# Hybrid encoder layer: head outputs kept in SBUF, scan operands laid out by step, local attention by bias class, stabilisers and norms moved into the first stage

## The chip, the cores and the metric

The kernel runs on one core of a Trainium2 chip. The metric is the device time of one execution in microseconds (us). A profile shows one execution: its span runs from the first to the last instruction.

## The reference

One layer of a bidirectional encoder over 2048 tokens of width 1024. All three head groups read one normalised input through one projection; then follow the output projection, cross attention to 256 memory tokens and a squared-ReLU MLP.

```python
h = rmsnorm(x, norm_mix_w[l])
(na_q, na_k, na_v, ml_q, ..., gd_b, gd_a) = jnp.split(h @ w_in[l], IN_OFFSETS, axis=-1)
y_na = neighbourhood_attention(na_q, na_k, na_v, na_rel_bias[l])    # 6 heads, window 8 x 16 on a 32 x 64 grid
y_ml = mlstm_mixer(...)                    # 4 heads; out = head_rms(h_fwd + h_bwd) * norm_w * sigmoid(o_pre)
y_gd = gated_deltanet_mixer(...)           # 6 heads; o = head_rms(o_fwd + o_bwd) * norm_w * silu(z)
x = x + jnp.concatenate([y_na, y_ml, y_gd], axis=-1) @ w_out[l]
x = x + memory_cross_attention(rmsnorm(x, ...), rmsnorm(mem, ...), w_xq[l], w_xkv[l], w_xo[l])
h = rmsnorm(x, norm_ffn_w[l])
x = x + jnp.square(jax.nn.relu(h @ w_ff1[l])) @ w_ff2[l]
# gdn_direction, one chunk of 64 tokens:
v_new = u_c - jnp.einsum('bhld,bhde->bhle', w_c, state)
o = jnp.einsum('bhld,bhde->bhle', qd_c, state) + jnp.einsum('bhls,bhse->bhle', a_c, v_new)
state = state * jnp.exp(gl_c)[..., None, None] + jnp.einsum('bhld,bhle->bhde', ks_c, v_new)
```

The mLSTM has the same form with a matrix memory and a running maximum (its stabiliser). Both scans run once forwards and once backwards, and the two outputs are added before the head norm.

## The kernel before

The kernel has three stages. `pass_a` normalises the input in four blocks of 512 tokens (`norm_in`), runs the projections as three-pass split GEMMs (the helper at L95: weights and activations are split into a high and a low part, `whi` and `wlo`), the convolution and gates of the gated DeltaNet (GDN), and its Gram matrices and inverses. GEMM work of the other groups is a generator, `fill`, advanced between steps of that chain. `norm_in(2)` and `norm_in(3)` were called between pieces of `fill`. What `pass_b` needs is written to DRAM: `sc_d`, `g_row`, `v_d`, `w_d` and `gd_c` for the GDN, `mlc_d`, `mlv_d` for the mLSTM, `nac_d`, `nav_d` for local attention, `gate_d` for the output gates.

`pass_b` interleaves four generators: 16 steps of the GDN scan (`gdn_scan`), 16 steps of the mLSTM scan one step later (`ml_scan`), local attention over 16 blocks of 128 tokens (`na`), and the head outputs (`heads_out`). A step handles 128 tokens of each direction: the forward scan takes tile m, the backward scan tile 15 - m. `load(m + 1)` is issued ahead of step m. Its DMAs all go through the SyncE queue, which runs in order. The scheduler moves instructions between generators, so the order on each engine is not that of the code. `ml_prep` computes the running-max stabilisers ahead of the mLSTM scan and writes rows `mx_row` and `ai_row`.

The two directions sit in the two halves of the 128 partitions (`CH[d]`). A row that all 64 partitions need, as `ge` or `me`, is read from DRAM once for each partition:

```python
nc.sync.dma_start(out=kb[CH[d]], in_=self.sc_d[d, t, :, :, 2].rearrange("c s h l -> s c h l"))
nc.sync.dma_start(out=ge[SR[d]], in_=self.g_row[t, :, d][None].broadcast_to([64, 2, 6, 64]))
```

Each step writes its outputs to `ho_d` in DRAM (L676 GDN, L886 mLSTM, GpSimd queue). A tile is complete when both directions have passed it, from step 8 on; `heads_out` then reloads both (`ob`, L690), loads the gate (`gz`, L692), adds (L694), normalises, transposes (L710), multiplies by the gate (L712) and stores to `y_d` (L713). In `na` a block loads its values with one DMA for four grid rows (L914; 24 or 32 columns of each row, so the source runs over 4 rows, then columns, then 384 values), its queries (L917) and, where its class is new, three bias tables (L908). The last stage is output projection, cross attention and MLP.

Of the kernel before, what the change touches and what calls it, by code (L numbers as in the profile page):

```python
# [38 lines left out]
class Trunk:  # L39
# [59 lines left out]
    def mix(self):  # L99

        tc, nc, I, dr = self.tc, self.nc, self.I, self.dr
        dt = lambda name, shape: dr.tile(shape, F32, name=name)
        self.y_d = [dt(f"y_d{b}", [8, P, 512]) for b in range(4)]
        self.gd_c = dt("gd_c", [9, P, T])
        self.gate_d = dt("gate_d", [5, P, T])
        self.ho_d = dt("ho_d", [16, P, 2, 640])
        self.mlc_d = dt("mlc_d", [4, P, T])
# [4 lines left out]
        self.sc_d = dt("sc_d", [2, 16, 2, 64, 3, 6, 64])  # L112
# [27 lines left out]
    def pass_a(self):  # L140

        with ExitStack() as st:
# [4 lines left out]
            self.np = pool("nin", 1)  # L147
# [14 lines left out]
            self.norm_in(1)  # L162
            for pr in range(2):
# [8 lines left out]
                fill = chain(self.ml_in(bs), self.na_kv(bs), self.na_q(bs), *(self.gdn_z((b,)) for b in bs)) if pr == 0 else chain(self.na_kv(bs), self.na_q(bs), self.ml_in(bs), self.gdn_z(bs))  # L172
                if pr == 0:
                    self.grams((0, 1, 2), fill)
                    inv = self.inv(0, (0, 1))
                    self.steps(inv, fill, I_FILL, 1)
                    self.grams((3, 4, 5, 6), fill)
                    self.steps(chain(inv, self.inv(1, (0, 1))), fill, I_FILL)
                    self.steps(fill, iter(()), 0, 34 - 14)
                    self.norm_in(2)  # L180
                    self.steps(fill, iter(()), 0)
                    self.norm_in(3)
# [23 lines left out]
    def pass_b(self):  # L206

        with ExitStack() as st:
# [9 lines left out]
            with self.pool("mlp", 1) as p:  # L218
                self.ml_prep(p)
# [102 lines left out]
    def gates(self, b):  # L322
# [76 lines left out]
    def gram(self, t):  # L399
# [55 lines left out]
        for d in range(2):  # L455
# [4 lines left out]
            nc.sync.dma_start(out=self.sc_d[d, t].rearrange("c s a h l -> (c s) (a h l)"), in_=sc.rearrange("p a h l -> p (a h l)"))  # L460
# [66 lines left out]
    def ml_in(self, blocks):  # L527

        nc, I, pool = self.nc, self.I, self.rp
        for ct in range(4):  # L530
            def put(ps, sl):
                t = pool.tile([P, 512], F32, name="rt")
                nc.scalar.activation(out=t, in_=ps, func=AF.Copy, scale=0.125 if ct < 2 else 1.0)
                nc.sync.dma_start(out=self.mlc_d[ct, :, sl], in_=t)
            yield from self.pair(I["w_ml"][ct], blocks, put)
# [68 lines left out]
    def gdn_scan(self, pool):  # L604
# [9 lines left out]
        def load(m):  # L614
# [5 lines left out]
            for d in range(2):  # L620
# [3 lines left out]
                nc.sync.dma_start(out=kb[CH[d]], in_=self.sc_d[d, t, :, :, 2].rearrange("c s h l -> s c h l"))  # L624
                nc.sync.dma_start(out=sc[CH[d], d, :, 0:2].rearrange("p c a h l -> p c (a h l)"), in_=self.sc_d[d, t, :, :, 0:2].rearrange("c s a h l -> s c (a h l)"))
# [19 lines left out]

        cur = load(0)
        for d in range(2):
            V.memset(cur[1][SR[d], d, d, 2], 0.0)
        evac = (V.tensor_copy, nc.scalar.copy)
        for m in range(16):  # L650
            nxt = load(m + 1) if m < 15 else None
            o = pool.tile([P, 2, 384], F32, name="o", bufs=1)
            wp, sc = cur
            for i in range(2):
# [19 lines left out]
                for d in range(2):  # L674
                    evac[1 - d](out=o[CH[cc[d]], d], in_=ps[CH[cc[d]], :384])
            nc.gpsimd.dma_start(out=self.ho_d[m, :, :, 256:640], in_=o)  # L676
# [3 lines left out]
    def heads_out(self, pool):  # L680
# [6 lines left out]
        for t in (7, 8, 6, 9, 5, 10, 4, 11, 3, 12, 2, 13, 1, 14, 0, 15):  # L687
            ob = pool.tile([P, 2, 10, 64], F32, name="ob")
            for d in range(2):
                nc.sync.dma_start(out=ob[:, d].rearrange("p h e -> p (h e)"), in_=self.ho_d[15 - t if d else t, :, d])  # L690
            gate = pool.tile([P, 5, P], F32, name="gz")
            nc.sync.dma_start(out=gate, in_=self.gate_d[:, :, P * t:P * t + P].rearrange("c p l -> p c l"))  # L692
            o = ob[:, 0]
            nc.gpsimd.tensor_tensor(out=o, in0=o, in1=ob[:, 1], op=ALU.add)  # L694
# [21 lines left out]
    def ml_prep(self, pool):  # L716
# [3 lines left out]
        self.mx_row = dr.tile([2, 2, 16, 4, 64], F32, name="mx_row")  # L720
# [8 lines left out]
        def trans(dst, src):  # L729
            ps = self.lps.tile([P, 512], F32, name="psl")  # L730
# [44 lines left out]
        nc.sync.dma_start(out=self.mx_row.rearrange("c d t h l -> (d t h) c l"), in_=mx)  # L775
        V.tensor_tensor(out=t0, in0=mr[:, :, 0:1].broadcast_to([P, 2, 64]), in1=mx, op=ALU.subtract)
        nc.scalar.activation(out=t0, in_=t0, func=AF.Exp)
        nc.sync.dma_start(out=self.ai_row.rearrange("d t h c l -> (d t h) (c l)"), in_=flat3(t0))
# [12 lines left out]
        for dst, src in ((self.cmx, rc), (self.wxx, t2)):  # L791
            ps = self.lps.tile([P, 512], F32, name="psl")
# [6 lines left out]
    def ml_scan(self, pool):  # L799
# [11 lines left out]
        def load(m):  # L811
# [7 lines left out]
            for d in range(2):  # L819
                t = m if d == 0 else 15 - m  # L820
                nc.sync.dma_start(out=kq[:, d], in_=self.mlc_d[:, :, P * t:P * t + P].rearrange("c p l -> p c l"))
                nc.sync.dma_start(out=e[CH[d]], in_=self.mx_row[None, :, d, t].broadcast_to([64, 2, 4, 64]))
                nc.sync.dma_start(out=r[CH[d], d].rearrange("p c h x -> p c (h x)"), in_=self.mlv_d[t].rearrange("(c s) h x -> s c (h x)", c=2))
                nc.sync.dma_start(out=qe[SR[d]], in_=self.mlc_d[0:2, :, P * t:P * t + P].rearrange("c (h e) l -> e (c h) l", h=2))
                nc.sync.dma_start(out=ge[SR[d]], in_=self.ai_row[d, t].rearrange("h c l -> (h c l)")[None].broadcast_to([64, 512]).rearrange("p (h l) -> p h l", l=P))
# [30 lines left out]
        for m in range(16):  # L856
            nxt = load(m + 1) if m < 15 else None
            o = pool.tile([P, 2, 4, 64], F32, name="mo", bufs=1)
            sc, r = cur
            for i in range(2):  # L860
# [22 lines left out]
                for d in range(2):  # L883
                    rows = CH[cc[d]]
                    V.tensor_tensor(out=o[rows, d], in0=pv[rows, :, 0:64], in1=ab[rows, :, None].broadcast_to([64, 4, 64]), op=ALU.mult)
            nc.gpsimd.dma_start(out=self.ho_d[m, :, :, 0:256], in_=o.rearrange("p i h e -> p i (h e)"))  # L886
# [3 lines left out]
    def na(self, pool):  # L890
# [3 lines left out]
        ks = pool.tile([P, 3, T], F32, name="nak", bufs=1)  # L894
        for j in range(3):
            nc.sync.dma_start(out=ks[:, j], in_=self.nac_d[3 + j])
        grid = lambda ap: ap.rearrange("p j (r c) -> p j r c", c=64)
        blocks = sorted(NA_BLOCKS, key=lambda k: (ORDER.index(k[0]), k[1]))
        bias = {}

        def load(i):
            rb, cb, r0, nr, c0, ncl, cls, first = blocks[i]
            if cls not in bias:
                bias.clear()
                bias[cls] = []
                for hp in range(3):
                    bt = pool.tile([P, 2, 480], F32, name="nab", bufs=4)
# [13 lines left out]
        for i, (rb, cb, r0, nr, c0, ncl, cls, first) in enumerate(blocks):  # L921
# [9 lines left out]
            for hp in range(3):  # L931
                pts = []
                for h in (2 * hp, 2 * hp + 1):
                    hb = slice(64 * (h % 2), 64 * (h % 2) + 64)
                    sp = self.nps.tile([P, 512], F32, name="psn")
                    nc.tensor.matmul(out=sp[:, :nk], lhsT=q[hb, hp], rhs=grid(ks)[hb, hp, r0:r0 + nr, c0:c0 + ncl], start=True, stop=True)  # L936
# [438 lines left out]
```

## Time and profile before

| | |
|---|---|
| median of 3 runs | 3932.8 us (3921.6 to 3935.67) |
| profiled execution | 3929.86 us |
| its span | 3928.0 us |
| mean granted TensorE clock | 0.917 of full speed |
| TensorE busy | 3493.0 us, 89% of the span |
| VectorE, ScalarE, GpSimd busy | 1742.0, 1129.1, 1483.8 us |
| DMA | 448.23 MB in 392918 packets |

Engines are PE (TensorE matmul), PEld (its weight loads), DVE (VectorE), ACT (ScalarE), POOL (GpSimd) and SP (SyncE, which here issues DMAs). An engine's idle time costs something only if the path that ends last runs through it. "L12" is line 12 of the kernel. "A <- B" in a wait reads: A waited for B. The DMA share is the mean busy share of 16 DMA engines.

### The profile page before, as it was taken

The numbers are of one execution on the slowest core, as the hardware profiler recorded it, in microseconds if no ns is written. First come the engines' busy times: TensorE is split into PE (matmuls) and PEld (weight loads), VectorE is DVE, ScalarE is ACT, GpSimd is POOL, SyncE is SP. The second block draws the span as 40 slices with busy tenths as digits, with TensorE's granted clock in tenths as the row PEclk, the third lists the DMA queues.
The fourth block names the chain that finished last, engine by engine and source line by source line (L and its number), as shares of the span: only waits on it lengthen the run. The fifth ranks groups of instructions, "written<-read, shape, count | busy, mean of one in ns | idle before, by whom it ended". The sixth has DMA issues, their size and how long they took to land.

```text
span 3928.0 us, 53839 instructions
## 1 busy us (share of the span) xinstructions
PE 3493.0 (89%) x21360; PEld 2812.2 (72%) x21360; DVE 1742.0 (44%) x3193; ACT 1129.1 (29%) x1989; POOL 1483.8 (38%) x921
## 2 busy tenths in 40 slices
PE   4988979888687777639999999999999999999998
PEld 3766767776465565438888887788888878888887
DVE  7868276671365655444434335422222262222224
ACT  3222322222232333213434334322222242222223
POOL 4242242534233333235445453433333353333333
PEclk8999989999687777659999999999999999999999
DMA  4475423865887787433232323311111141111112
GB/s 137 114 207 122 120 89 107 255 145 143 184 209 188 180 212 211 123 117 111 97 129 97 126 94 121 113 49 54 46 46 46 44 134 62 46 49 51 49 53 86
DMA packets 392918, 448.23 MB, mean 114 GB/s; under 512 B 151562, under 2 KB 296410, under 8 KB 390618
## 3 DMA queue, kind: packets, MB, share of 16 engines
q1 hardware_dynamic: 389050, 432.72, 38.9%
q0 software_dynamic: 3616, 12.06, 1.0%
q8 instruction: 169, 2.77, 0.3%
q14 instruction: 83, 0.68, 0.1%
HBM read 342.19 MB, written 102.50 MB: 113 GB/s over the span
## 4 chain that ended last, share of the span: by engine, by line
PE 61%; DMA 10%; DVE 7%; issue 3%; SPq 2%; ACT 2%; POOL 1%; DVEq 0%; POOLq 0%; ACTq 0%
PE psg L95 34%; PE psa L95 20%; DVE acc L295 1%; DMA me<-mx_row 1%; PE psn L936 1%; DMA mkq<-mlc_d 1%; DMA ge<-g_row 1%; DVE tv L482 1%; PE psn L945 1%; DVE x L483 1%; PE psy L955 1%; DMA nab<-in_nab 1%; DMA wp<-w_d 1%; DMA sc<-v_d 1%; DMA ob<-ho_d 1%
## 5 line engine op out<-in xcount | busy, mean ns | idle before, releaser
L979 POOL TENSOR_TENSOR wlo<-wraw,whi 128x1024 fp32r<-128x1024 f32 (+1 forms) x383 | 777.4, 2030 | 1400.2 <-ACT whi L977 1362.2
L95 PE MATMUL psg<-acta,whi 128*128 128x512 f32 (+1 forms) x3008 | 956.4, 399 | 4.3 <-ACT acta L1118 3.2
L95 PE MATMUL psg<-actb,whi 128*128 128x512 f32 (+1 forms) x2752 | 840.4, 387 | 43.2 <-ACT actb L260 17.5
L977 ACT CAST whi<-wraw 128x1024 fp32r<-128x1024 f32 (+2 forms) x399 | 355.0, 890 | 1233.1 <-PE psa L95 556.0
L95 PEld LDWEIGHTS psg<-acta,whi 128*128 128x128 f32 (+1 forms) x3008 | 570.6, 191 | 127.6 <-ACT acta L1118 3.9
L95 PE MATMUL psa<-ht,whi 128*128 128x512 f32 x2048 | 638.8, 395 | 0.8 <-ACT whi L977 0.8
L95 PEld LDWEIGHTS psg<-actb,whi 128*128 128x128 f32 x2752 | 514.2, 191 | 151.2 <-ACT actb L260 18.1
L95 PE MATMUL psg<-acta,wlo 128*128 128x512 f32 (+1 forms) x1504 | 595.7, 397 | 1.1 <-POOL wlo L979 1.1
L95 PE MATMUL psg<-actb,wlo 128*128 128x512 f32 (+1 forms) x1376 | 531.8, 387 | 3.2 <-POOL wlo L979 3.2
L95 PEld LDWEIGHTS psa<-ht,whi 128*128 128x128 f32 x2048 | 384.0, 188 | 95.3 <-ACT whi L977 1.6
L95 PE MATMUL psa<-ht,wlo 128*128 128x512 f32 x1024 | 400.7, 396 | 0.5 <-POOL wlo L979 0.5
L1210 DVE TENSOR_TENSOR fr<-fr 128x512 f32<-128x512 f32 x128 | 168.2, 1314 | 496.4 <-ACT fr L1209 496.4
L1223 DVE TENSOR_TENSOR xb<-psa,xb 128x512 f32<-128x512 f32 x256 | 175.7, 691 | 476.1 <-PE psa L95 476.1
L95 PEld LDWEIGHTS psg<-acta,wlo 128*128 128x128 f32 (+1 forms) x1504 | 286.8, 191 | 63.7 <-POOL wlo L979 2.3
L95 PEld LDWEIGHTS psg<-actb,wlo 128*128 128x128 f32 x1376 | 262.9, 191 | 55.4 <-POOL wlo L979 4.9
L1213 POOL TENSOR_TENSOR ht<-fr,ht 128x512 fp32r<-128x512 f32 x128 | 169.0, 1320 | 249.2 <-ACT ht L1212 247.9
L95 PEld LDWEIGHTS psa<-ht,wlo 128*128 128x128 f32 x1024 | 192.2, 188 | 47.3 <-POOL wlo L979 1.7
L632 POOL TENSOR_TENSOR sc<-qe,ge 64x768 f32<-64x768 f32 x32 | 65.0, 2032 | 215.8 <-DMA wp<-w_d 79.6
L1006 DVE TENSOR_TENSOR ss<-ss,sqt 128x512 f32<-128x512 f32 (+1 forms) x91 | 121.9, 1340 | 45.5 <-ACT sqt L1005 42.6
L295 DVE SCALAR_TENSOR_TENSOR acc<-pad,vecs,acc 128x512 f32<-128x512 f32 (+2 forms) x144 | 135.5, 955 | 2.7
L1212 ACT CAST ht<-fr 128x512 fp32r<-128x512 f32 x128 | 79.4, 621 | 181.2 <-DVE fr L1210 181.1
L945 PE MATMUL psn<-ident,nas 128*96 128x128 f32 (+1 forms) x336 | 75.1, 352 | 52.3 <-ACT nas L941 52.2
(376 smaller groups left out, 3991.3 us busy)
## 6 DMA issues: line engine op xcount, KB each, us to landing
wraw<-in_w_ff SPq DMA_DIRECT2D x72, 512.0 KB
wraw<-in_w_ff SPq DMA_DIRECT2D x144, 256.0 KB
sc_d<-sc SPq DMA_DIRECT2D x32, 576.0 KB
wraw<-in_w_out SPq DMA_DIRECT2D x32, 512.0 KB
wraw<-in_w_xq SPq DMA_DIRECT2D x32, 512.0 KB
wraw<-in_w_xo SPq DMA_DIRECT2D x32, 512.0 KB
wraw<-in_w_gd SPq DMA_DIRECT2D x24, 512.0 KB
sc<-sc_d SPq DMA_DIRECT2D x32, 384.0 KB
```

The source lines that it names most:

```text
L95: nc.tensor.matmul(out=out, lhsT=a(k), rhs=b(k), start=(i == 0), stop=(i == n - 1))
L295: V.scalar_tensor_tensor(out=acc[:, :n], in0=pad[:, p0 + j:p0 + j + n], scalar=cw(j), in1=acc[:, :n], op0=ALU.mult, op1=ALU.add)
L482: V.tensor_tensor(out=tv, in0=m[:, j + 1:32, j:j + 1].broadcast_to([2 * N, n, j]), in1=m[:, j:j + 1, 0:j].broadcast_to([2 * N, n, j]), op= ...
L632: G.tensor_tensor(out=sc[SR[d], d, :, 0], in0=qe[SR[d]].rearrange("p h (c l) -> p c h l", c=2), in1=ge[SR[d]], op=ALU.mult)
L945: nc.tensor.transpose(out=tp[:n, P * j:P * j + P], in_=s[:, kt * j:kt * j + n], identity=self.ident)
L977: nc.scalar.copy(out=hi, in_=raw)
L979: (lo_eng or nc.gpsimd).tensor_tensor(out=lo, in0=raw, in1=hi.bitcast(F32), op=ALU.subtract)
L1006: nc.vector.tensor_tensor(out=ss, in0=ss, in1=sq, op=ALU.add)
L1210: V.tensor_tensor(out=r, in0=r, in1=r, op=ALU.mult)
L1212: S.copy(out=ht[:, 0], in_=r)
L1213: G.tensor_tensor(out=ht[:, 1], in0=r, in1=ht[:, 0].bitcast(F32), op=ALU.subtract)
L1223: V.tensor_tensor(out=xs[nb][:, j], in0=ps, in1=xs[nb][:, j], op=ALU.add)
```

## The change

Head outputs: `ho_d` goes. A tile `acc` [128, 16, 10, 64] in SBUF takes the outputs; steps 0 to 7 write, later ones add. `heads_out` works on `acc` in place, and its gate tile has one buffer, not two.

Scan operands: `kb` moves to a DRAM tensor of its own, `kb_d` [2, 16, 64, 2, 6, 64], and the gate rows get a second copy `g_st` [2, 16, 2, 6, 64]. `mx_row` and `ai_row` are laid out by direction and step. For each step `kb`, `ge`, `me` and `mge` are one load for both directions. `mlc_d` is laid out by step.

Local attention: blocks are sorted by row class so that equal classes follow each other, keys are held for 24 of the 32 grid rows and reloaded at block 8, two logit matmuls are issued before their softmax work, some pools have a buffer less.

First stage: `norm_in(2)` and `norm_in(3)` run inside the generator `fill_first`; `ml_prep` runs inside `pass_a`; the first scan load is issued ahead of the rest of `pass_b`.

```diff
@@ pass_a
             with self.tc.high_priority(offset=500):
                 self.norm_in(0)
-            self.norm_in(1)
+                self.norm_in(1)
...
+                    norms.close()
+                    with self.pool("mlp", 1) as p:
+                        self.ml_prep(p)
...
+    def fill_first(self):
+        yield from self.ml_in((0, 1))
+        yield from self.na_kv((0, 1))
+        yield from self.na_q((0,))
+        yield from self.gdn_z((0,))
+        self.norm_in(2)
+        yield from self.na_q((1,))
+        yield from self.gdn_z((1,))
+        self.norm_in(3)
@@ pass_b
+            self.acc = pool("acc", 1).tile([P, 16, 10, 64], F32, name="acc")
             scan = self.gdn_scan(pool("scan", 2))
+            next(scan)
@@ gates
+            for t in range(4):
+                for d in range(2):
+                    nc.sync.dma_start(out=self.g_st[1 - d, 4 * b + t, c], in_=row[12 * t + 6 * d:12 * t + 6 * d + 6, 64 * c:64 * c + 64])
@@ grams
+            for c2 in range(2):
+                nc.sync.dma_start(out=self.kb_d[d, t, :, c2], in_=sc[64 * c2:64 * c2 + 64, 2])
@@ gdn_scan, load(m) and step
-                nc.sync.dma_start(out=kb[CH[d]], in_=self.sc_d[d, t, :, :, 2].rearrange("c s h l -> s c h l"))
-                nc.sync.dma_start(out=ge[SR[d]], in_=self.g_row[t, :, d][None].broadcast_to([64, 2, 6, 64]))
+            both(kb.rearrange("p c h l -> p (c h l)"), self.kb_d.rearrange("d t s c h l -> (d t) s (c h l)")[m:32 - m:31 - 2 * m])
+            both(ge.rearrange("p c h l -> p (c h l)"), self.g_st.rearrange("d t c h l -> (d t) (c h l)")[15 - m:17 + m:2 * m + 1, None].broadcast_to([2, 64, 768]))
+        def both(out, in_):
+            nc.sync.dma_start(out=out, in_=in_)
...
-            nc.gpsimd.dma_start(out=self.ho_d[m, :, :, 256:640], in_=o)
+                    o = self.acc[rows, (m, 15 - m)[d], 4:10].rearrange("p h x -> p (h x)")
+                    if m < 8:
+                        evac[1 - d](out=o, in_=ps[rows, :384])
+                    else:
+                        V.tensor_tensor(out=o, in0=ps[rows, :384], in1=o, op=ALU.add)
@@ heads_out
-            ob = pool.tile([P, 2, 10, 64], F32, name="ob")
-            for d in range(2):
-                nc.sync.dma_start(out=ob[:, d].rearrange("p h e -> p (h e)"), in_=self.ho_d[15 - t if d else t, :, d])
-            gate = pool.tile([P, 5, P], F32, name="gz")
+            gate = pool.tile([P, 5, P], F32, name="gz", bufs=1)
-            nc.gpsimd.tensor_tensor(out=o, in0=o, in1=ob[:, 1], op=ALU.add)
+            o = self.acc[:, t]
@@ ml_scan, load(m)
-                nc.sync.dma_start(out=e[CH[d]], in_=self.mx_row[None, :, d, t].broadcast_to([64, 2, 4, 64]))
+            nc.sync.dma_start(out=e.rearrange("p c h l -> p (c h l)"), in_=self.mx_row.rearrange("d t c h l -> (d t) (c h l)")[m:32 - m:31 - 2 * m, None].broadcast_to([2, 64, 512]))
+            nc.sync.dma_start(out=ge.rearrange("p h l -> p (h l)"), in_=self.ai_row.rearrange("d t h c l -> (d t) (h c l)")[15 - m:17 + m:2 * m + 1, None].broadcast_to([2, 64, 512]))
@@ na
-        blocks = sorted(NA_BLOCKS, key=lambda k: (ORDER.index(k[0]), k[1]))
+        blocks = sorted(NA_BLOCKS, key=lambda k: ((1, 0, 0, 2)[k[0]], k[6], k[0], k[1]))
+            if i == 8:
+                ks, row = keys(((0, 12), (20, 32)))
```

The slice `[m:32 - m:31 - 2 * m]` over the merged axis (direction, tile) picks two entries, tile m of the forward direction and tile 15 - m of the backward one. They are the outermost dimension of the source; the 64 rows come second.

On the SyncE queue, before, in the middle of the scans: loads of one direction stand beside those of the other (`x2`: two in a row; the shape is that of the destination).

```order
L624 DMA kb<-sc_d 64x2x384 x2
L823 DMA mr__9321<-mlv_d 64x2x260 x2
L627 DMA qe<-gd_c 64x6x128
L628 DMA ge<-g_row 64x2x384
L627 DMA qe<-gd_c 64x6x128
L628 DMA ge<-g_row 64x2x384
```

The same queue after, at about the same place:

```order
L644 DMA qe<-gd_c 64x6x128 x2
L666 DMA kb<-kb_d 128x1x768
L666 DMA ge<-g_st 128x1x768
L847 DMA mr__9444<-mlv_d 64x2x260 x2
L641 DMA wp<-w_d_85 64x768
L641 DMA wp<-w_d_91 64x768
L849 DMA mqe<-mlc_d 64x2x128 x4
L851 DMA mge<-ai_row 128x1x512
```

`kb`, `ge` and `mge` are single loads of 128 partitions now; `mqe` has become four.

On the same queue near the end of the scan stage, before: reloads of the outputs (L690) stand between stores and gate loads.

```order
L690 DMA ob<-ho_d 128x640
L713 DMA y_d_68<-gz 128x5x128
L692 DMA gz<-gate_d 128x5x128
L690 DMA ob<-ho_d 128x640
L713 DMA y_d_71<-gz 128x5x128
L692 DMA gz<-gate_d 128x5x128
L690 DMA ob<-ho_d 128x640 x3
```

After, there:

```order
L735 DMA y_d_68<-gz 128x5x128
L715 DMA gz<-gate_d 128x5x128
L735 DMA y_d_71<-gz 128x5x128
L715 DMA gz<-gate_d 128x5x128
L1122 DMA mt<-in_memT 128x2048
L735 DMA y_d_68<-gz 128x5x128
L715 DMA gz<-gate_d 128x5x128
```

Store and gate load alternate, and the load of the memory tokens (`mt`), which stood at the start of the stage, is among them.

On TensorE in the first stage, before, at the second half of the last input norm, `norm_in(3)`: sum of squares (L76) and the broadcast of its root (L86) stand next to each other, and the first GEMM on the new activations (`actb`) follows.

```order
L95 MATMUL psg<-acta,whi 128x512 x2
L95 MATMUL psg<-acta,wlo 128x512
L76 MATMUL psm<-ones,ss 128x1 x2
L86 MATMUL psm<-ident,rs 128x128 x2
L95 MATMUL psg<-actb,whi 128x512
L95 MATMUL psg<-acta,whi 128x512 x2
```

After, around the broadcast of that half:

```order
L95 MATMUL psg<-acta,wlo 128x512
L95 MATMUL psg<-acta,whi 128x512 x2
L86 MATMUL psm<-ident,rs 128x128 x2
L95 MATMUL psg<-acta,wlo 128x512
L95 MATMUL psg<-acta,whi 128x512 x2
L95 MATMUL psg<-acta,wlo 128x512
```

Its L76 stands 18 rows of the order ahead of this L86, and the first GEMM on `actb` 16 rows behind it, with GEMMs on `acta` in between.

## Rows read from the trace of the kernel before

**Rows 1.** Page part 2: DMA share in tenths, 40 slices of the span.

```profile
DMA  4475423865887787433232323311111141111112
```

**Rows 2.** Windows by stage: length, busy PE, PEld, DVE, ACT, POOL, clock, DMA share, GB/s.

```profile
960.00:1740.00 780.00, 534.17 (x6499) 391.71 (x6495) 403.19 (x1024) 234.45 (x582) 242.05 (x179) 0.71 0.71 182
1020.00:1520.00 500.00, 393.31 (x5339) 297.35 (x5341) 284.71 (x679) 179.35 (x450) 171.83 (x129) 0.78 0.78 192
1520.00:1740.00 220.00, 114.47 (x891) 76.27 (x890) 106.34 (x317) 44.48 (x107) 66.56 (x48) 0.60 0.50 150
1740.00:3928.00 2188.00, 2140.76 (x9752) 1764.24 (x9752) 743.08 (x934) 631.18 (x1030) 878.88 (x529) 0.99 0.24 78
```

**Rows 3.** Waits in 960 to 1740: us in total, times, longest us.

```profile
DVE me L826 <- DMA me<-mx_row: 77.1, 13, 13.0
...
ACT ge L629 <- DMA ge<-g_row: 46.3, 10, 11.1
```

**Rows 4.** The chain of waits, start of the scans and near 1204: start us, us.

```profile
1022.02 13.06 DMA mt<-in_memT
...
1204.71 13.14 DMA nav<-nav_d
```

**Rows 5.** Windows in which few DMA engines are busy; columns as in rows 2.

```profile
1205.00:1208.00 3.00, 3.00 (x45) 2.10 (x42) 2.14 (x6) 0.47 (x1) 0.00 (x0) 1.00 0.26 87
2600.00:3000.00 400.00, 400.00 (x1738) 325.94 (x1737) 97.71 (x112) 81.43 (x124) 133.84 (x90) 1.00 0.16 49
2066.00:2070.00 4.00, 4.00 (x20) 3.35 (x19) 0.00 (x0) 1.41 (x2) 1.28 (x1) 1.00 0.31 121
```

**Rows 6.** DMA issues in 960 to 1740: count, KB each, us to landing.

```profile
kb<-sc_d SPq DMA_DIRECT2D x32, 192.0 KB
...
ge<-g_row SPq DMA_DIRECT2D x32, 192.0 KB
ho_d<-o POOLq DMA_DIRECT2D x16, 384.0 KB, 6.8
...
nav<-nav_d SPq DMA_DIRECT2D x22, 192.0 KB
me<-mx_row SPq DMA_DIRECT2D x32, 128.0 KB
...
mge<-ai_row SPq DMA_DIRECT2D x32, 128.0 KB
ho_d<-mo POOLq DMA_DIRECT2D x16, 256.0 KB, 3.9
...
nav<-nav_d SPq DMA_DIRECT2D x28, 144.0 KB
...
nav<-nav_d SPq DMA_DIRECT2D x6, 108.0 KB
...
ob<-ho_d SPq DMA_DIRECT2D x32, 320.0 KB
```

**Rows 7.** Waits near the stage's end, PE and SP queue: us, times, longest.

```profile
PE psl L710 <- issue: 30.8, 2, 16.0
...
PE psl L710 <- DVE ob L706: 22.6, 4, 17.6
...
SPq L692 <- DMA y_d<-gz: 30.7, 9, 6.2
```

**Rows 8.** PE waits in 500 to 550: us in total, times, longest.

```profile
PE psm L86 <- POOL rs L68: 8.6, 1, 8.6
PE psg L95 <- ACT actb L260: 7.5, 1, 7.5
PE psm L76 <- DVE ss L249: 4.2, 1, 4.2
```

**Rows 9.** Waits of the SP queue in 100 to 960: us, times, longest.

```profile
SPq L299 <- DVE acc L298: 120.6, 25, 9.0
```

More of the change, by code (lines that the diff above doesn't have):

```diff
@@ L111, in mix @@
         self.g_row = dt("g_row", [16, 2, 2, 6, 64])
-        self.sc_d = dt("sc_d", [2, 16, 2, 64, 3, 6, 64])
+        self.sc_d = dt("sc_d", [2, 16, 2, 64, 2, 6, 64])
+        self.kb_d = dt("kb_d", [2, 16, 64, 2, 6, 64])
+        self.g_st = dt("g_st", [2, 16, 2, 6, 64])
         self.v_d = dt("v_d", [16, 2, 64, 6, 64])
@@ L171, in pass_a @@
                     self.gates(b)
-                fill = chain(self.ml_in(bs), self.na_kv(bs), self.na_q(bs), *(self.gdn_z((b,)) for b in bs)) if pr == 0 else chain(self.na_kv(bs), self.na_q(bs), self.ml_in(bs), self.gdn_z(bs))
+                fill = self.fill_first() if pr == 0 else chain(self.na_kv(bs), self.na_q(bs), self.ml_in(bs), self.gdn_z(bs))
                 if pr == 0:
@@ L533, in put @@
                 nc.scalar.activation(out=t, in_=ps, func=AF.Copy, scale=0.125 if ct < 2 else 1.0)
-                nc.sync.dma_start(out=self.mlc_d[ct, :, sl], in_=t)
+                nc.sync.dma_start(out=self.mlc_d[sl.start // P:sl.stop // P, :, ct].rearrange("j p l -> p j l"), in_=t.rearrange("p (j l) -> p j l", l=P))
             yield from self.pair(I["w_ml"][ct], blocks, put)
@@ L651, in gdn_scan @@
             nxt = load(m + 1) if m < 15 else None
-            o = pool.tile([P, 2, 384], F32, name="o", bufs=1)
             wp, sc = cur
@@ L774, in ml_prep @@
         V.tensor_tensor(out=mx, in0=pm, in1=mr[:, :, 0:1].broadcast_to([P, 2, 64]), op=ALU.max)
-        nc.sync.dma_start(out=self.mx_row.rearrange("c d t h l -> (d t h) c l"), in_=mx)
+        for ch in range(2):
+            nc.sync.dma_start(out=self.mx_row[:, :, ch].rearrange("d t h l -> (d t) h l"), in_=mx[:, ch])
         V.tensor_tensor(out=t0, in0=mr[:, :, 0:1].broadcast_to([P, 2, 64]), in1=mx, op=ALU.subtract)
         nc.scalar.activation(out=t0, in_=t0, func=AF.Exp)
-        nc.sync.dma_start(out=self.ai_row.rearrange("d t h c l -> (d t h) (c l)"), in_=flat3(t0))
+        for d in range(2):
+            nc.sync.dma_start(out=self.ai_row[1 - d].rearrange("t h c l -> (t h) (c l)"), in_=flat3(t0)[R[d]])
         V.tensor_tensor(out=t0, in0=rb, in1=mx, op=ALU.add)
@@ L884, in ml_scan @@
                     rows = CH[cc[d]]
-                    V.tensor_tensor(out=o[rows, d], in0=pv[rows, :, 0:64], in1=ab[rows, :, None].broadcast_to([64, 4, 64]), op=ALU.mult)
-            nc.gpsimd.dma_start(out=self.ho_d[m, :, :, 0:256], in_=o.rearrange("p i h e -> p i (h e)"))
+                    o = self.acc[rows, (m, 15 - m)[d], 0:4]
+                    if m < 8:
+                        V.tensor_tensor(out=o, in0=pv[rows, :, 0:64], in1=ab[rows, :, None].broadcast_to([64, 4, 64]), op=ALU.mult)
+                    else:
+                        mo = pool.tile([P, 4, 64], F32, name="mo", bufs=1)
+                        V.tensor_tensor(out=mo[rows], in0=pv[rows, :, 0:64], in1=ab[rows, :, None].broadcast_to([64, 4, 64]), op=ALU.mult)
+                        V.tensor_tensor(out=o, in0=o, in1=mo[rows], op=ALU.add)
             cur = nxt
@@ L893, in na, with keys @@
         V, G = nc.vector, nc.gpsimd
-        ks = pool.tile([P, 3, T], F32, name="nak", bufs=1)
-        for j in range(3):
-            nc.sync.dma_start(out=ks[:, j], in_=self.nac_d[3 + j])
+        def keys(parts):
+            ks = pool.tile([P, 3, 24 * 64], F32, name="nak", bufs=1)
+            at = 0
+            row = {}
+            for a, b in parts:
+                row.update({r: at + r - a for r in range(a, b)})
+                nc.sync.dma_start(out=ks[:, :, 64 * at:64 * (at + b - a)], in_=self.nac_d[3:6, :, 64 * a:64 * b].rearrange("j p l -> p j l"))
+                at += b - a
+            return ks, row
+        ks, row = keys(((4, 28),))
         grid = lambda ap: ap.rearrange("p j (r c) -> p j r c", c=64)
-        blocks = sorted(NA_BLOCKS, key=lambda k: (ORDER.index(k[0]), k[1]))
+        blocks = sorted(NA_BLOCKS, key=lambda k: ((1, 0, 0, 2)[k[0]], k[6], k[0], k[1]))
         bias = {}
@@ L926, in na @@
                 nxt = load(i + 1)
+            if i == 8:
+                ks, row = keys(((0, 12), (20, 32)))
+            k0 = row[r0]
             kt = 4 * ncl
@@ L931, in na @@
             for hp in range(3):
[L932 to L936, printed above, removed]
+                pts, sps = [], [self.nps.tile([P, 512], F32, name="psn") for _ in range(2)]
+                for sp, hb in zip(sps, (slice(0, 64), slice(64, 128))):
+                    nc.tensor.matmul(out=sp[:, :nk], lhsT=q[hb, hp], rhs=grid(ks)[hb, hp, k0:k0 + nr, c0:c0 + ncl], start=True, stop=True)
+                for sp, h in zip(sps, (2 * hp, 2 * hp + 1)):
                     s = pool.tile([P, 480], F32, name="nas", bufs=3)
```

40 lines of the change are left out of this document (17 added, 23 removed).

## Prediction

> **What bounds the kernel now.** I read the page's slices first. From the tenth of the 40 slices to the sixteenth the DMA digits stand at 7 and 8, while before and after them they are lower [rows 1]. That is the scan stage. The table by windows then gives its numbers [rows 2]: from 1020 to 1520 us TensorE is busy 393 of 500 us at a clock of 0.78, and the 16 DMA engines are busy 0.78 of the time on average. After 1520 both fall (114 of 220 us, share 0.50): there the last mLSTM steps, the head outputs and their reloads run one after another. The rest of the program, 1740 to 3928, is dense TensorE work at clock 0.99 (2141 of 2188 us), which the change leaves alone. So the change is won or lost between 960 and 1740, and a little near 500.
>
> In that stage the operands of the two scans come late: VectorE waits 77.1 us for `me`, ScalarE 46.3 us for `ge` [rows 3]. These are two of the four loads that the change rebuilds, so how their transfers are spread over the DMA engines decides.
>
> A mean over 16 engines hides an uneven load. The `nav` loads of local attention show it. Their source pattern goes over four grid rows first, then the columns of a row. The chain waits 13.14 us for `nav` loads of at most 192 KB each [rows 4, 6], and in 1205 to 1208, when little else is in flight, the DMA share is 0.26 with 87 GB/s [rows 5]. 0.26 x 16 = 4.2 engines, each at 87 / 4.2 = 20.9 GB/s. I read this as: a transfer whose pattern starts with four pieces runs on four engines.
>
> The Trainium skill ("DMA: Bandwidth & Descriptors", "Why a DMA increments its semaphore by 16 and not by 1") states this as a rule: the slowest dimension of size above 1 on either side is looked at, and the number of engines is the largest count up to 16 that divides both; its table for kernel authors adds that a small outermost dimension confines the whole DMA. The 4.2 engines of the `nav` window agree with the four that it gives there. It also says that the lowest-numbered engines are taken, which no row here shows.
>
> **The hot engines before.** The stage moved 182 GB/s x 780 us = 142 MB at share 0.71, so a mean engine was busy 554 us and moved 142 MB / 16 in that time, 16.0 GB/s [rows 2]. The `nav` loads are 22 x 192 + 28 x 144 + 6 x 108 KB = 9.1 MB [rows 6]. If the same four engines carry them, each has 2.28 MB, 109 us at 20.9 GB/s; 27 us of it is already in the mean, so these four were busy 554 + 82 = 636 of 780 us and idle 144. Between 1020 and 1520 they had up to 390 + 82 = 472 of 500 us, that is 0.94: close to full. That they are the same four each time is my reading.
>
> **What the change does to them.** `kb`, `ge`, `me` and `mge` were two loads each per step, one per direction, with 64 rows outermost. Now each is one load for both directions, with the two directions outermost in the source and 64 rows inside. The destination is 128 partitions, but the source begins with 2. By the reading above such a load runs on two engines. Their bytes: (15 + 16) x 384 KB for `kb` and `ge` (the last `kb` load covers neighbouring blocks and merges to 128 rows) and 32 x 256 KB for `me` and `mge`, half of it on each engine: 31 x 64 x 3072 B + 32 x 64 x 2048 B = 10.29 MB per engine. The price per byte comes from rows with long pieces: 2066 to 2070 gives 121 / (0.31 x 16) = 24.4 GB/s per engine, the `nav` window 20.9, and the long stretch 2600 to 3000 gives 49 / (0.16 x 16) = 19.1 [rows 5]. So 422, 492 or 539 us. I take 422, since rows of 2 and 3 KB are nearer to the weight rows of the first than to the 1.5 KB of `nav`. That is 26 us per step on two engines, where a step now takes 500 / 16 = 31 us in all.
>
> The same engines carry their sixteenth of everything else. Removed: the output writes 16 x (384 + 256) KB and the reloads 32 x 320 KB, together 21.0 MB; the old form of the four operands, 64 x 192 + 64 x 128 KB = 21.0 MB [rows 6]; and about 2 MB net of bias tables less key reloads (nine bias loads fewer, 1.6 MB of keys more). Left are 142 - 44 = 98 MB, 6.1 MB per engine: 383 us at the stage's 16.0 GB/s, 251 us at 24.4. With engines 2 to 15 relieved, pieces should move faster than now but not as in an empty stretch, so I take the middle, 317. `nav` adds 70 to 82, say 76. The two engines then have 317 + 76 + 422 = 815 us of work; the ends are 251 + 70 + 422 = 743 and 383 + 82 + 539 = 1004.
>
> **Length of the stage.** To this I add the time in which they idle: 144 us now, most of it in the drain. There TensorE waits 30.8 + 22.6 us at the transposes of the head outputs [rows 7], behind the chain output write, reload, POOL addition. With the outputs kept in SBUF that chain goes, 53 us; I count 95 us of idle time (ends 50 and 144). So the stage takes 815 + 95 = 910 us in place of 780: +130 (ends +13 and +368).
>
> **Norms of the first stage.** The second and third input norm now start inside the filling work. Of the waits 4.2 + 8.6 + 7.5 us [rows 8] up to 20.3 us can go. The new TensorE order puts about 80 GEMM matmuls between statistics and use, but VectorE and POOL still have the same chain among gates and convolutions: I take -10 (ends -20 and 0). The first norms (offset 500 now around both) keep their order and give nothing.
>
> **Costed at nothing.** The mLSTM stabilisers move into the first stage, with about 130 small store issues for `kb_d` and `g_st` and 512 B store pieces for the mLSTM operands. SyncE spends 120.6 us of that stage waiting at one store line alone [rows 9], so it has room; uncovered it would be 0 to +15. The memory tokens' load leaves the start, where the chain waits 13.06 us for it [rows 4], and comes near the end, in the SyncE queue between head-output stores: -13 to +13, taken as 0, since the mLSTM loads that now stand ahead of the first scan loads use the time. 64 accumulating additions fall on VectorE, which has 780 - 403 = 377 us idle in the stage [rows 2], over 5 us for each. Logits in pairs and the merged bias classes touch waits on `nas` and bias loads that hide behind the scan steps; 0, or -15 if the scans weren't late.
>
> **Sum.** 3929.9 (the profiled execution; the median of the three runs is 3932.8, 3 us more) + 130 - 10 = 4050 us.
>
> **Rivals.**
> A. The paired loads spread over all engines. Then the two hot engines vanish, 23 MB less is moved, and TensorE's order bounds the middle: it cannot go under the 393 us that TensorE is busy, and halfway from 500 is 445: -55. The drain gives its 53 back, the norms 10, the start 13: -131, about 3800 (3720 to 3870). For it: bytes really fall. Against it: the `nav` window, where a load with a short outermost count reached four engines only. 0.13.
> B. Confined, but all else moves at 24.4 GB/s and the drain shrinks to 50 us idle: 793 us of stage, +13 - 10, so 3933. It needs both ends at once. 0.08.
> C. Spread, but the single `gz` buffer decides. Each gate load must wait until the store of the tile before has landed. With two buffers this wait is already 30.7 us in 9 times, at most 6.2 [rows 7]; with one, 15 tiles may expose a store and a load, 2 x 6.2 us, with every later load queued behind on SyncE: +186 - 131 = +55, so 3985. It turns slower from 131 / 15 = 8.7 us per tile. Against it: the sigmoid gates of early tiles are fetched while the scans run. 0.05.
>
> **How the numbers follow.** The forecast has 0.74, its own range 3950 to 4170 (low rates of the common share, or 492 us for the pairs). The 80% range has to take in case B and most of the upper bounds, and leaves out A: 3900 to 4190. A difference within 0.5% (3913 to 3953) is about what a measurement of this kernel can't tell from none. Faster is A, 0.13; same is B, 0.08; slower is the forecast and C, 0.79.
>
> **What would show it.** In the after profile: middle steps of about 40 us, not 31, with a DMA share falling to about 0.5 though loads are waited for; waits on `kb`, `ge`, `me` or `mge` at the head of the lists, with landings over 10 us; stretches with a share near 2 / 16 and 50 GB/s. The transposes' waits gone. Near 500 us no gaps of 8 us on TensorE. The forecast is wrong if those loads run at a share above 0.5, or if the middle steps are at 31 us or less; then A or C holds, and the waits at the gate loads tell which.

## The result: 5.1% slower, and the profile after

| | before | after |
|---|---|---|
| median | 3931.0 us (4 runs) | 4129.4 us (4 runs, 4125.5 to 4135.5) |
| ratio | | 1.0509, 95% interval 1.0486 to 1.0533 |
| span of the profiled execution | 3928.0 us | 4127.3 us |
| DMA bytes | 448.23 MB | 426.79 MB |

The forecast was 4050 us, the range 3900 to 4190. The way and the place were right; the size was 120 us where 198 were lost (199 of the span). Bytes did fall by 21 MB, and the kernel still became slower.

Where the 199 us of span lie is read from windows cut at the same events: the first and the last output matmul of the GDN scan, and the start of the dense tail; 960 us is a fixed time. Before (columns: length, busy PE, PEld, DVE, ACT, POOL, clock, DMA share, GB/s):

```profile
960.00:1026.00 66.00, 32.12 (x349) 23.13 (x347) 12.69 (x29) 12.36 (x30) 4.51 (x3) 0.53 0.84 211
1026.00:1520.00 494.00, 387.57 (x5264) 292.30 (x5266) 284.16 (x678) 177.62 (x447) 170.98 (x129) 0.78 0.78 192
1520.00:1761.00 241.00, 123.79 (x925) 83.83 (x924) 116.94 (x334) 53.54 (x124) 78.31 (x59) 0.60 0.49 149
1761.00:3928.00 2167.00, 2131.45 (x9718) 1756.68 (x9718) 732.47 (x917) 622.12 (x1012) 867.12 (x517) 0.99 0.24 78
```

After, the same cuts, with the stretch of the norms first and two idle microseconds of TensorE last; they answer to [rows 2, 5]:

```profile
500.00:550.00 50.00, 43.32 (x185) 34.73 (x184) 41.33 (x57) 13.07 (x18) 21.77 (x7) 0.97 0.27 80
960.00:1059.00 99.00, 42.02 (x383) 29.94 (x380) 18.81 (x46) 14.31 (x36) 17.20 (x14) 0.55 0.42 109
1059.00:1790.00 731.00, 448.24 (x5401) 331.52 (x5401) 313.81 (x747) 182.83 (x466) 146.09 (x95) 0.69 0.43 116
1790.00:1958.00 168.00, 65.80 (x595) 49.75 (x595) 94.22 (x261) 31.90 (x70) 45.00 (x33) 0.59 0.38 120
1958.00:4127.00 2169.00, 2132.22 (x9718) 1757.12 (x9718) 731.35 (x918) 623.33 (x1014) 870.20 (x519) 0.99 0.24 78
...
1370.00:1372.00 2.00, 0.00 (x0) 0.00 (x0) 0.00 (x0) 0.00 (x0) 0.00 (x0) 0.50 0.13 52
```

The start grew by 33 us, the 16 scan steps by 237 (30.9 to 45.7 us each), the drain shrank by 73, and the tail kept its length: 33 + 237 - 73 + 2 = 199. In the scan steps the mean DMA share fell from 0.78 to 0.43 while the loads were waited for more than before. That pair of facts is what an uneven load looks like in a mean. The last row shows it bare: TensorE idle, a share of 0.13, that is 0.13 x 16 = 2.1 engines, and 52 GB/s, 25 GB/s for each of the two. Counted over the scan steps in the DMA records of the trace, exactly two packets are under way at once in 255 of the 731 us.

The waits in 960 to 1958, against [rows 3] (us in total, times, longest):

```profile
ACT ge L647 <- DMA ge<-g_st: 272.4, 16, 28.3
DVE me L852 <- DMA me<-mx_row: 195.9, 16, 38.8
```

46.3 and 77.1 us have become 272.4 and 195.9. The chain of waits near step 7 (start us, us):

```profile
1355.37 19.48 DMA ge<-g_st
1375.31 13.52 DMA me<-mx_row
1405.67 21.48 DMA ge<-g_st
...
1459.64 18.38 DMA ge<-g_st
```

A load of 384 KB at 52 GB/s takes 7.6 us alone; here the chain waits 18 to 21 us for it. `kb`, of the same size and kind, is issued just ahead of it. The DMA view of 1370 to 1390 (40 slices of 0.5 us; the first row is the share in tenths):

```profile
DMA  1111297746757821211111111138971492111100
GB/s 49 55 49 55 72 214 280 259 109 207 279 98 139 340 74 49 90 49 48 48 52 51 50 49 49 53 90 252 277 225 29 125 295 76 51 49 51 45 20 16
```

Runs of 1 with 48 to 55 GB/s fit the paired loads alone: in 1370 to 1372 every packet under way has 3072 bytes, the row length of `kb` and `ge`. In the runs of 7 to 9 other loads are under way on many engines, and they are soon done.

### The profile page after: what moved, and what is told of

It reads as the page before. It is cut to its first block, busy times and chain, and to the rows that moved or that the text cites. A ratio compares the mean times of both kernels' runs of the same rounds, so it can differ in the third digit from the quotient of the medians.

```text
span 4127.3 us, 53735 instructions
## 1 busy us (share of the span) xinstructions
PE 3515.8 (85%) x21360; PEld 2830.8 (69%) x21360; DVE 1770.1 (43%) x3241; ACT 1122.2 (27%) x1976; POOL 1435.5 (35%) x876
## 2 busy tenths in 40 slices
DMA packets 376610, 426.79 MB, mean 103 GB/s; under 512 B 150872, under 2 KB 277544, under 8 KB 374696
## 4 chain that ended last, share of the span: by engine, by line
PE 56%; DMA 13%; DVE 4%; SPq 3%; issue 2%; POOL 2%; ACT 1%; DVEq 0%; POOLq 0%; ACTq 0%
PE psg L95 31%; PE psa L95 19%; DMA ge<-g_st 4%; DMA me<-mx_row 3%; DMA wp<-w_d 1%; DMA y_d<-gz 1%; PE psn L977 1%; SPq L953 1%; PE psy L997 1%; PE psn L987 1%; DMA sc<-sc_d 1%; SPq L846 1%; DMA nav<-nav_d 0%; PE pss L688 0%; POOL wlo L1021 0%
## 5 line engine op out<-in xcount | busy, mean ns | idle before, releaser
L1021 POOL TENSOR_TENSOR wlo<-wraw,whi 128x1024 fp32r<-128x1024 f32 (+2 forms) x386 | 773.1, 2004 | 1367.0 <-ACT whi L1019 1328.7
L853 POOL TENSOR_TENSOR me<-me,gm 128x512 f32<-128x512 f32 x16 | 21.1, 1320 | 456.9 <-DVE me L852 414.4
L308 DVE SCALAR_TENSOR_TENSOR acc<-pad,vecs,acc 128x512 f32<-128x512 f32 (+2 forms) x144 | 143.8, 1012 | 2.8
L997 PE MATMUL psy<-nap,nav 96*64 96x128 f32 (+2 forms) x672 | 89.3, 349 | 52.1 <-ACT nap L990 47.8
```

The lines of the kernel that those rows point to most:

```text
L308: V.scalar_tensor_tensor(out=acc[:, :n], in0=pad[:, p0 + j:p0 + j + n], scalar=cw(j), in1=acc[:, :n], op0=ALU.mult, op1=ALU.add)
L997: nc.tensor.matmul(out=yp[64 * e:64 * e + 64, P * hp:P * hp + P], lhsT=vw[:n, j, 128 * hp + 64 * e:128 * hp + 64 * e + 64], rhs=pts[e][:n, ...
L1021: (lo_eng or nc.gpsimd).tensor_tensor(out=lo, in0=raw, in1=hi.bitcast(F32), op=ALU.subtract)
```

## The experiments

Ratios are against the kernel before on the same chip. Kernels compared with each other in us ran in part on different chips, on which the kernel before took 3925 to 3932 us, so a few us between two of them say nothing.

**The pairs split: the cause of the loss.** This version is called e1 below. The edit, for `kb` and `ge` (for `me` and `mge` likewise):

```diff
         def both(out, in_):
-            nc.sync.dma_start(out=out, in_=in_)
+            for d in range(2):
+                nc.sync.dma_start(out=out[CH[d]], in_=in_[d])
```

> The changed kernel with the four paired operand loads split again into one load per direction, so that 64 rows are the outermost dimension of the source; all else of the change stays. Theory (two DMA engines carry the paired loads and bound the scans): the 10.3 MB per engine are spread, the scan step falls from 45.7 us to 31 us or less and the time to 3760 to 3870 us. Rival (the rest of the change slows it: single gate buffer, key reload, later memory tokens, other order): the time stays above 4050 us and the step above 42 us.

Measured: 3879.7 us, ratio 0.9875 (0.9855 to 0.9895). The same bytes with 64 rows outermost make the change 250 us faster and turn it from a loss to a gain of 1.2%. Exactly two packets are under way at once in 9 of its 523 us of scan steps, not in 255 of 731. Its windows, cut at the same events, and its waits in the scan steps:

```profile
960.00:1027.00 67.00, 45.11 (x415) 32.38 (x417) 19.62 (x43) 16.48 (x41) 20.59 (x14) 0.55 0.75 181
1027.00:1550.00 523.00, 408.54 (x5436) 304.63 (x5435) 315.54 (x754) 183.51 (x465) 146.46 (x94) 0.77 0.65 163
1550.00:1711.00 161.00, 68.20 (x581) 51.04 (x577) 91.72 (x257) 28.45 (x65) 44.50 (x32) 0.57 0.37 118
```

```profile
ACT ge L647 <- DMA ge<-g_st: 46.0, 10, 11.5
DVE me L855 <- DMA me<-mx_row: 39.7, 9, 11.8
```

The start is back at 67 us and the drain keeps its gain. But the steps are 32.7 us each, not 31 or less, though the DMA share is a sixth lower (0.65 against 0.78): the first part of the expectation held, the step length missed it by a little.

**Half of the pairs split.** First `kb` and `ge` only (e2), then `me` and `mge` only (e3); the edits are the two halves of the one above.

> Only kb and ge are loaded per direction; me and mge stay paired (32 x 64 x 2048 B on each of two engines, 172 us at 24.4 GB/s). Theory: these two engines have about 317 + 76 + 172 = 565 us of work, less than the 636 us that four engines had in the kernel before, so they no longer bound: 3800 to 3920 us. If time went with the paired bytes in proportion, without a bound, it would be 4129 less 58% of the gain of splitting all four.

Measured: 3979.5 us, ratio 1.0132 (1.0115 to 1.0150).

> Only me and mge are loaded per direction; kb and ge stay paired (31 x 64 x 3072 B on each of two engines, 250 us at 24.4 GB/s). Theory: about 317 + 76 + 250 = 643 us of work on two engines, as much as the hot engines had before: 3880 to 3980 us. In proportion to the bytes it would be 4129 less 42% of the gain of splitting all four.

Measured: 4054.4 us, ratio 1.0331 (1.0308 to 1.0354). Both came out slower than the theory of a bound said. The bytes of `kb` and `ge` are 59% of the paired ones (250 of 422 us; the 58% and 42% written ahead of the runs are a little off). Splitting them gains 150 of the 250 us (60%), splitting the other 41% gains 75 (30%). So at neither amount of paired work tried, 172 and 250 us on each engine, did the two engines do no harm; the loss goes about with the paired bytes. The waits of the scan steps point to how. With `me` and `mge` paired (e2):

```profile
DVE me L853 <- DMA me<-mx_row: 107.8, 12, 20.3
ACT ge L647 <- DMA ge<-g_st: 91.3, 12, 17.1
```

With `kb` and `ge` paired (e3):

```profile
ACT ge L647 <- DMA ge<-g_st: 242.1, 14, 25.3
...
DVE me L854 <- DMA me<-mx_row: 60.5, 6, 30.6
```

In the first, `ge` is spread over all engines and still waited for 91.3 us, against 46.0 with no pair left; in the second `me` is spread and waited for 60.5 against 39.7. The reading that fits: a load that is spread is done when its last piece is, and some of its pieces stand behind the pair on the two engines. No row names the engine of a piece.

The traces show a second way as well: the issue itself is held up. These are SyncE's instructions that issue `ge` in the scan steps, of the kernel after and of e1 (SPq is SyncE's queue; duration in ns: least, median, most):

```profile
L666 SPq DMA_DIRECT2D ge<-g_st x14: 517/2093/5105, 1065.6 to 1698.3; - x14
L667 SPq DMA_DIRECT2D ge<-g_st x28: 445/594/1636, 1031.3 to 1479.6; - x28
```

What stands behind such an issue in SyncE's queue is issued later too. Added up over the scan steps, SyncE's DMA issues took 391 us for 369 of them after, 353 for 393 in e3, 263 for 401 in e2 and 247 for 420 in e1. How the loss divides between the two ways was not tried.

**The pairs on another queue.** The edit for `kb` and `ge` (for `me` and `mge` likewise):

```diff
         def both(out, in_):
-            nc.sync.dma_start(out=out, in_=in_)
+            nc.gpsimd.dma_start(out=out, in_=in_)
```

> The paired loads stay paired but are issued by GpSimd on its own queue. Theory A (the SyncE queue always takes the same two engines, and a paired load on another queue takes two others or changing ones): the paired bytes leave the two engines that also carry their share of everything else; the time falls by over 100 us, to 3850 to 4020. Theory B (the paired load itself, 8 us long on two engines wherever they are, is waited for, or the two engines are the same): 4080 to 4180.

Measured: 3967.2 us, ratio 1.0102 (1.0085 to 1.0120), 162 us under the change as made, with the same access patterns. The scan steps and their DMA queues (q1 is SyncE's, q0 GpSimd's; packets, MB, share of the 16 engines' time):

```profile
1035.00:1597.00 562.00, 405.24 (x5236) 302.71 (x5235) 303.79 (x705) 175.58 (x448) 175.67 (x139) 0.74 0.61 145
```

```profile
q1 hardware_dynamic: 60478, 63.45, 48.3%
q0 software_dynamic: 25952, 16.96, 12.1%
```

17 MB, the pairs, now go through GpSimd's queue, and the mean share rises from 0.43 to 0.61 with nearly the same bytes (427.0 MB in the whole program, 426.8 without the edit). The time is that of theory A. The two queue rows bear out that the pairs were spread over more than two engines: 0.121 x 16 x 562 = 1088 us of engine time would be 544 us on each of any two fixed engines, and a sixteenth of the other queue's work, taken as even, is 0.483 x 562 = 271 us more; 815 us don't fit into 562. The Trainium skill ("DMA: Bandwidth & Descriptors", "Why a DMA increments its semaphore by 16 and not by 1") says why it may be so: from SyncE a load that runs on fewer than 16 engines takes the lowest-numbered ones, from GpSimd a consecutive group that moves on from load to load. The time agrees; which engines carried a piece stands in no row. The edit also takes the pairs out of SyncE's own queue, whose 297 issues took 200 us in these steps; what that alone is worth was not separated.

**The four-engine loads that were there before.** If two engines are the trouble, the `nav` loads should cost in the kernel before as well.

```diff
-                nc.sync.dma_start(out=vw[:rows * ncl, j], in_=src)
+                for a in range(rows):
+                    nc.sync.dma_start(out=vw[a * ncl:a * ncl + ncl, j], in_=src[a])
```

> The kernel before, with each nav load cut into one load per grid row (24 or 32 rows of partitions outermost, in place of 4 grid rows). Theory (four engines, 0.94 busy with nav, were the bound of the scans before): the 82 us that nav costs these four beyond its even share go, and the scans get 20 to 60 us shorter: 3870 to 3910. Rival (the even load of 0.78 or the order on the engines bounds the scans, and the some 150 loads more only cost SyncE issue time): 3925 to 3970.

Measured: 3886.5 us, ratio 0.9902 (0.9880 to 0.9923): 38 us faster with some 150 DMAs more. The time is as expected, its place isn't:

```profile
960.00:1008.00 48.00, 18.72 (x254) 15.67 (x256) 5.31 (x20) 7.57 (x15) 4.85 (x3) 0.52 0.89 214
1008.00:1514.00 506.00, 414.61 (x5428) 308.44 (x5425) 303.41 (x726) 188.59 (x477) 179.03 (x133) 0.79 0.82 202
1514.00:1718.00 204.00, 106.90 (x782) 73.50 (x778) 102.92 (x290) 46.17 (x103) 72.86 (x56) 0.59 0.49 149
```

The start is 18 us shorter and the drain 37; the scan steps are 12 longer. So the middle of the scans gained nothing from it: there the four hot engines don't show as what ended a step.

On top of the split pairs (e1), `nav` was moved to GpSimd's queue instead (e6; `nc.gpsimd.dma_start` in the same line).

> As e1_all16 (3880 us), with the nav loads issued by GpSimd, whose short loads took changing engines in e5_poolq. Theory (what nav puts on four fixed engines still delays the other loads): 10 to 40 us faster than e1, 3840 to 3870. Rival (nav no longer matters once the pairs are split, or GpSimd's issue time costs as much): 3870 to 3900.

Measured: 3846.3 us, ratio 0.9808 (0.9782 to 0.9833), 33 us under e1. Here the steps did get shorter: its last output matmul starts at 1511 us, 38 us ahead of e1, its first 1 us ahead.

**The single gate buffer** (rival C).

```diff
-                    V.scalar_tensor_tensor(out=gate[:, j], in0=ps[...], scalar=nw[:, j:j + 1], in1=gate[:, j], ...)
+                    V.scalar_tensor_tensor(out=o[:, 2 * j:2 * j + 2].rearrange("p a b -> p (a b)"), in0=ps[...], scalar=nw[:, j:j + 1], in1=gate[:, j], ...)
...
-            nc.sync.dma_start(out=self.y_d[...], in_=gate)
+            nc.sync.dma_start(out=self.y_d[...], in_=o.rearrange("p (c a) b -> p c (a b)", a=2))
```

> As e1_all16 (3880 us), with the gated product written back into acc and stored from there, so that the single gate buffer is free at the multiplication and the next gate load needn't wait for the store to land. Theory (in the drain each tile exposes a store, about 2.5 us, ahead of the gate load): the wait of the gate load for the store goes, 8 to 25 us faster, 3855 to 3872. Rival (the drain waits for the mLSTM steps anyway): 3875 to 3885.

Measured: 3863.3 us (3856.8 to 3878.1), ratio 0.9848 (0.9819 to 0.9877). The median is 16 us under e1, but the two intervals overlap (e1 reaches down to 0.9855): a gain as expected is likely, but not shown by this run alone.

**The logits in pairs.** On e1, each logit matmul was put back ahead of its own softmax (the allocation of `sp` and the matmul inside the loop over the two heads).

> As e1_all16 (3880 us), with the two logit matmuls of a head pair no longer issued one after the other but each ahead of its own softmax, as before the change. If the pairs, which hold both psn buffers, are why the scan step did not get shorter than before (522 against 493 us for 16 steps): 3840 to 3870. If they help as meant: 3885 to 3910. If they are hidden: 3870 to 3890.

Measured: 3876.5 us, ratio 0.9866 (0.9839 to 0.9894): no difference from e1 that is clear of the noise.

**The norms alone on the kernel before.**

```diff
-                fill = chain(self.ml_in(bs), ...) if pr == 0 else ...
+                fill = self.fill_first() if pr == 0 else ...
...
-                    self.steps(fill, iter(()), 0, 34 - 14)
-                    self.norm_in(2)
                     self.steps(fill, iter(()), 0)
-                    self.norm_in(3)
```

> The kernel before with one part of the change alone: the second and third input norm called inside the filling generator. As predicted for this part: 0 to 20 us faster, about 10, so 3905 to 3930 and near 3915. Rival (the gaps near 500 us go, but the inverses behind them set the end of the stage): 3920 to 3935.

Measured: 3891.0 us, ratio 0.9895 (0.9876 to 0.9915): 41 us, four times the forecast of this part, and mostly not at the place forecast. Two stretches of the first stage before, that of the norms and a later one:

```profile
500.00:550.00 50.00, 29.90 (x110) 24.32 (x110) 36.64 (x50) 13.06 (x15) 24.33 (x8) 0.73 0.22 76
650.00:800.00 150.00, 133.49 (x782) 109.56 (x783) 86.38 (x227) 33.84 (x50) 66.13 (x33) 0.90 0.72 211
```

With the norms in the generator, the same two, and the start, steps and drain of the scan stage:

```profile
500.00:550.00 50.00, 32.07 (x132) 25.24 (x130) 33.47 (x48) 12.45 (x15) 19.48 (x8) 0.80 0.27 85
650.00:800.00 150.00, 143.45 (x861) 117.39 (x861) 91.87 (x228) 34.23 (x51) 72.62 (x36) 0.94 0.71 212
960.00:1011.00 51.00, 30.33 (x239) 19.84 (x241) 7.17 (x26) 11.45 (x28) 6.13 (x4) 0.52 0.84 198
1011.00:1498.00 487.00, 375.22 (x5285) 285.97 (x5285) 295.15 (x692) 180.71 (x454) 174.13 (x132) 0.81 0.81 198
1498.00:1721.00 223.00, 111.09 (x878) 75.34 (x876) 109.16 (x316) 47.30 (x110) 71.62 (x56) 0.62 0.50 144
```

Near 500 us TensorE is still idle for 18 of 50 us, 2 less than before; from 650 to 800 it is busy 10 us more. The scans start 15 us earlier, the steps take 7 us less and the drain 18. The new order shifts what comes later; why the steps and the drain gain was not tried.

The counterpart: e1 with the norms called at their old places.

> As e1_all16 (3880 us, 46 us under before), but with the second and third input norm called where the kernel before calls them. The norms alone gained 41 us on the kernel before (b2_norms). If that gain is additive, 3910 to 3930, and all the rest of the change with pairs split (outputs in SBUF, 21 MB less, order, stabilisers in the first stage) is worth about 5 us. If the rest makes its own gain and the norms only part of it, 3880 to 3905.

Measured: 3895.8 us, ratio 0.9931 (0.9903 to 0.9958). The norms are worth 16 us in the changed kernel, not 41. The rest of the change with the pairs split is worth about 3925 - 3896 = 29 us. Alone the two parts give 41 and 29 us, 70 in sum; together, in e1, they give 46. Near 500 us the gap is back:

```profile
500.00:550.00 50.00, 32.49 (x127) 26.70 (x128) 34.70 (x50) 11.26 (x12) 21.85 (x8) 0.76 0.22 74
```

In e1 TensorE is busy 43.4 us of this stretch, so 11 of the 16 us lie there.

**A version that beats both.** e8 is e1 with `nav` on GpSimd's queue and the product written back into `acc`; e10 adds the logits not in pairs.

> The split pairs with both further edits: nav issued by GpSimd and the gated product written back into acc. If the two gains (34 and 16 us against e1_all16) add, 3825 to 3840. If they cover the same wait, 3840 to 3850.

Measured: 3838.3 us, ratio 0.9766 (0.9745 to 0.9788). The edits save 41 us on e1, inside the first case, though less than 34 + 16, and the interval overlaps that of e6 (0.9782 to 0.9833) at its edge.

> As e8_both with the logit matmuls not in pairs. On e1_all16 that moved 3 us at most; with the loads early the order on TensorE could count more. Pairs hidden: within 10 us of e8_both. Pairs in the way: 10 to 30 us faster.

Measured: 3807.9 us, ratio 0.9693 (0.9669 to 0.9717): 30 us under e8, the upper end of the second case. What was worth 3 us at most on e1 counts here; that the earlier loads are the reason was argued ahead of the run and not tried by itself. This is the fastest kernel, 124 us under the one before and 321 under the change as made. Its start, steps and drain:

```profile
960.00:1019.00 59.00, 48.12 (x438) 33.44 (x437) 16.58 (x37) 16.66 (x41) 20.55 (x17) 0.55 0.85 200
1019.00:1460.00 441.00, 351.57 (x5246) 268.45 (x5244) 310.88 (x712) 168.22 (x421) 169.93 (x134) 0.85 0.78 183
1460.00:1640.00 180.00, 118.87 (x819) 82.00 (x820) 108.88 (x307) 51.06 (x117) 53.55 (x42) 0.62 0.50 145
```

27.6 us per step at a granted clock of 0.85. TensorE is busy 351.6 us with about as many matmuls as in the kernel before (387.6 at clock 0.78).

## Why the prediction was right, and by how much it missed

- **Confinement to two engines.** Right, and shown: a share of 0.13 with 52 GB/s while nothing else runs, and 250 us back when only the outermost dimension of the sources changes. The price per byte of the pairs when alone, 24.4 GB/s per engine, was right too (25).
- **The sum of the hot engines' work.** The step that fell short. I put the common share at 317 us, midway between the stage's own rate and that of an empty stretch, expecting relieved engines to move faster. Over the stage the after kernel moved 109 to 120 GB/s at a share of 0.38 to 0.43; the scan steps give 116 / (0.43 x 16) = 16.9 GB/s per engine, barely above the 16.0 of before. With 383 us, the upper end, the sum is 383 + 82 + 422 + 95 = 982 us for the stage; from 960 to the start of the tail it took 998 (801 before, of which my 780 left out the last 21). That this comes so near is in part luck, as the next point and the drain show.
- **A bound, and so a threshold.** The idea behind the sum was too simple. By it e2, with 172 us of pairs in place of 422, would be 250 us faster than the kernel after, and e3, with 250, 172 us; they were 150 and 75. e2 should have lost nothing; it lost 100 us against e1. Beside paired loads, loads that are spread come later too, and about 250 / 422 = 0.6 us were lost per microsecond of paired work on an engine.
- **The hot engines before.** That `nav` costs time in the kernel before was right (38 us). That it bounds the middle of the scans at 0.94 was not borne out: the gain fell on the start and the drain.
- **The drain.** Shorter by 73 us, but not as I counted (49 of 144 idle us). 58 of the 73 are TensorE work that stands elsewhere now: the drain had 925 matmuls and 123.8 us of busy TensorE before, 595 and 65.8 after. Most of the missing ones are of local attention (into tiles `psn` and `psy`, 332 before, 127 after), and run in the start and the steps now. TensorE's idle time in the drain fell from 117 to 102 us only. And the waits at the transposes did not go. Of the 53 us in [rows 7], 30.8 had no releaser that the profile shows and 22.6 waited for the normalisation on VectorE (L706); the chain of write, reload and addition was my reading. After, in 1790 to 1958, they wait nearly as long for the same normalisation:

```profile
PE psl L732 <- DVE acc L728: 49.3, 9, 12.9
```

```profile
SPq L735 <- DVE gz L734: 40.6, 7, 14.6
SPq L715 <- DMA y_d<-gz: 17.4, 9, 2.4
```

  The gate load waits 2.4 us at most for the store, 17.4 in all. Rival C's 8.7 us per tile was far off. What the outputs kept in SBUF are worth by themselves was not tried.
- **The norms.** The gaps of [rows 8] went in the changed kernel (TensorE is busy 43.3 of 50 us there, 29.9 before), and 11 us lie there, as forecast. Yet -10 was too little: -16 there, -41 alone, where most of the gaps stayed. Of the 41, 25 come in the steps and the drain and are not explained.
- **The start.** Costed at nothing; it took 33 us more. With the pairs split it took 1 us more, so this is the same cause: the first loads of both scans are pairs too. The fixed cut at 960 us hides a gain that was lost again: the last matmul of the inverses in the first stage starts at 1006 us before, 977 after and 985 in e1, the first output matmul of the scan at 1027, 1059 and 1027.
- **Rival A, the transfers spread.** Made true by e1, it came to 3880, not 3800. The drain is 80 us shorter and the steps 29 us longer, in part because work moved out of the drain (TensorE busy 124 us before, 68 in e1) and into the steps (388, 409) and the start (32, 45). Together they gained 51 us where rival A counted 55 + 53. 21 MB less did not shorten the steps; they took 32.7 us each until `nav` moved (e6) and the logits were no longer paired (e10).

## What to carry to other kernels

A mean DMA share can't tell a free DMA system from one in which two engines carry most of the work: where a load is waited for at a low share, divide GB/s by share and look for stretches at 1/16 or 2/16. Before loads are merged into one, look at what becomes the outermost dimension on either side; here four operands, each brought by two loads with 64 rows outermost in place of one load with the two directions outermost, gave back 250 us. And a few confined loads cost about in proportion to their bytes here, with no amount tried that was free. A stage that gets shorter may only have handed its work on: compare its matmuls and busy time, not its length alone.

## What the runs showed that was not expected

- The same confined load costs less from another queue: issued by GpSimd, pairs lost 87 us against the split form (3967 against 3880), issued by SyncE 250.
- Part gains did not add: 41 us for the norms alone became 16, and the unpaired logits, worth 3 us at most on one version, were worth 30 on a faster one.
- A few engines can stay hot at a modest mean: with the pairs on two engines the kernel moved 116 GB/s in the scan steps; with the pairs split, 163.
